# First token block's attention chain in another bank, the filter's mean from one sum, a longer filter, weights loaded a step ahead

## The chip, the core and the metric

One core of a Trainium2 chip runs the kernel. The metric is the device time of one execution in microseconds; the time of a kernel is the median of its runs. TensorE is PE below, VectorE DVE, ScalarE ACT, GpSimd POOL and SyncE SP.

## The reference

One layer over 2048 tokens of 1024 channels, float32. An RMSNorm, one projection to 2816 columns, three mixers side by side, one output projection with the residual, a second RMSNorm, a squared-ReLU MLP with the residual, and a final RMSNorm:

```python
p = h @ w_in                                   # h = rmsnorm(x)
y_a = a_b * _causal_dwconv(a_c * a_h, w_conv_a)         # width 3
g = b_glu[..., :256] * jax.nn.sigmoid(b_glu[..., 256:])
g = _causal_dwconv(g, w_conv_b) + b_conv_b              # width 31
y_b = jax.nn.silu(_layernorm(g, ln_b_g, ln_b_b))        # over 256 channels
# 8 heads of 64, strictly causal, no softmax
z = einsum("bhqd,bhkd->bhqk", qb, kb) * scale
log_beta = log_sigmoid(z); log_1m = where(mask, log_beta - z, 0)
suffix = cumsum(log_1m, axis=3, reverse=True) - log_1m
a = where(mask, exp(log_beta + suffix), 0);  o = a @ vb
x = x + concat([y_a, y_b, y_c]) @ w_out
x = x + square(relu(rmsnorm(x) @ w_ff1)) @ w_ff2;  return rmsnorm(x)
```

## The kernel before, in words

Channels lie on the 128 partitions, tokens along the free axis in four blocks of 512. Each float32 product is made of three matmuls on parts: an operand is split into a rounded part "hi" (ACT copy) and the rest "lo" (a subtraction on DVE or POOL), and `mm3` (lines 99 to 107) adds hi x hi, lo x hi and hi x lo in one bank.

Phase 1 projects. `p_start` makes the first products, then `p_half(0)` treats token blocks 0 and 1 and `p_half(1)` blocks 2 and 3 (numbered by `tb`). Units of 256 columns come in the order G (the width-31 mixer), A (width-3 mixer), K, Q, V. A group of 24 matmuls fills one of three banks "d"; `p_evac` takes it out on DVE (sig, g, ac, u, ya, kq by unit), so the group three later needs the evacuation.

Beside the projections run generators, called sides. `weave` advances each by its share: a tuple says how many units of cost it has, and between which steps of the projections it is spread. A half has some 230 steps.
- `mixer_b`: the width-31 filter, 31 DVE instructions per 128 channels and token block (lines 450 and 452) into the bank "c"; then the LayerNorm: the mean of 256 channels as two matmuls with a constant matrix (line 461), the squares, a column sum (`colsum`), the root on POOL (`rsqrt`, line 118), and its spread back over the partitions by matmuls (`spread`, line 134). A `yield 1.8` separates steps.
- `attention` of token block 0 (i = 0) in half 1. `a_pass1` makes three score tiles z per head (lines 522, 523; ACT's sigmoids at 536 and 537 take them out, POOL masks them) and products R of the complements; `a_cross_a` (lines 610 to 637) turns R over (616), scans it (618), multiplies on (627, 631) and ends with line 635: the transposed products T. `a_pass2` turns T back into the bank "q" (653), multiplies the scores by it (656), splits them and makes eight matmuls "o" with V (701). `attention` runs pass 1 of one head and pass 2 of the one before in turn. Scores and the chain share two banks "z".
- `pre_split` in half 1: 24 pieces of w_out and w1 are loaded raw (five buffers), split into wph and wpl (ACT line 88, POOL line 90; two buffers of wph) and stored for later use.

Phase 2, from some 556 us on, has four blocks of output projection and MLP (`block`), with the attention of token blocks 1 to 3 woven in.

The program's order is not the last word: the framework's scheduler orders the instructions of each engine by its own timing model, and `high_priority` pulls some ahead. Each engine then works in order. DMAs are issued from SP's queue, some from ACT's and POOL's.

Of the kernel before, what the change touches and what calls it, by code (L numbers as in the profile page):

```python
# [7 lines left out]
F32 = mybir.dt.float32  # L8
F32R = mybir.dt.float32r
I32 = mybir.dt.int32  # L10
AF = mybir.ActivationFunctionType
ALU = mybir.AluOpType
# [3 lines left out]
P = 128  # L16
S = 2048
D = 1024
DC = D // P
TB = 512  # L20
H = 8
HD = 64
# [46 lines left out]
class Trunk:  # L69
# [78 lines left out]
    def consts(self, ctx):  # L148
# [6 lines left out]
        nc.scalar.dma_start(t, a["g_attn"].rearrange("(d p) -> p d", p=P))  # L155
# [24 lines left out]
    def vectors(self):  # L180
        nc, tc, a, c = self.nc, self.tc, self.a, self.c
        for name in ("g_ffn", "g_final"):
            t = c.tile([P, DC], F32, name=name)
            self.dma(t, a[name].rearrange("(d p) -> p d", p=P))
            self.gvec[name] = t
        self.wa = c.tile([P, 2, 3], F32, name="wa")
        self.dma(self.wa, a["w_conv_a"].rearrange("(c p) k -> p c k", p=P))
        self.wb = c.tile([P, 2, 31], F32, name="wb")
        self.dma(self.wb, a["w_conv_b"].rearrange("(c p) k -> p c k", p=P))
        self.vb = {}  # L190
        for name in ("b_conv_b", "ln_b_g", "ln_b_b"):
            t = c.tile([P, 2], F32, name=name)
            self.dma(t, a[name].rearrange("(c p) -> p c", p=P))
            self.vb[name] = t
# [246 lines left out]
    def mixer_b(self, hf):  # L441
        nc = self.nc
        for tb in (2 * hf, 2 * hf + 1):
# [13 lines left out]
            for _ in range(3):  # L457
                yield 1.8
            mean = self.psum("ps_mean", "c")
            for c in range(2):  # L460
                nc.tensor.matmul(mean, self.avg, acc[c], start=c == 0, stop=c == 1)
# [11 lines left out]
            for _ in range(4):  # L473
                yield 1.8
# [71 lines left out]
    def a_pass1(self, g):  # L546
# [37 lines left out]
        yield 1  # L584
        tot = self.a_cross_a(g, Rd, None)
# [24 lines left out]
    def a_cross_a(self, g, R, seed):  # L610
# [3 lines left out]
        X = self.ps.tile([P, TB], F32, name="ps_t", tag="z", bufs=self.banks["z"])  # L614
# [24 lines left out]
    def a_pass2(self, g):  # L639
# [39 lines left out]
        tmp = pool.tile([P, TB], F32, name="otmp", tag="om", bufs=ab["om"])[:HD]  # L679
        nc.scalar.activation(tmp, o[HD:P], AF.Copy)  # L680
# [3 lines left out]
        nc.vector.tensor_tensor(self.yc[HD * (h % 2) : HD * (h % 2) + HD], o[0:HD], tmp, op=ALU.add)  # L684
# [27 lines left out]
    def attention(self, groups):  # L712
# [3 lines left out]
        for n in range(len(groups) + 1):  # L716
# [6 lines left out]
            live1, live2 = g is not None, prev is not None  # L723

            lag = 0 if prev and prev["i"] else 2
            while live1 or live2:
                if live2 and (not live1 or (d2 + lag) * max(n1, 1) <= d1 * max(n2, 1)):
                    try:
                        next(p2)
                        d2 += 1  # L730
                        yield 0.5
                    except StopIteration:
                        live2 = False
                elif live1:
                    try:
                        next(p1)
                        d1 += 1
                        yield 0.5
                    except StopIteration:
                        live1 = False  # L740

                if nxt is None and d1 >= 1 and n + 1 < len(groups):
                    nxt = self.a_queries(*groups[n + 1])
                if nxt and "Kd" not in nxt and d1 >= 3:
                    self.a_keys(nxt)
# [19 lines left out]
    def pre_split(self):  # L765

        for name, c, q in self.presplit:
            raw = self.w_raw(self.unit_source(name, c, q))
# [263 lines left out]
    def build(self):  # L1032
        tc = self.tc
        with ExitStack() as ctx:
# [6 lines left out]
            with ExitStack() as c1:  # L1041
# [13 lines left out]
                weave(self.p_half(0), [(Side(self.mixer_b(0)), 115, 20, 225, True), (Side(self.x_norms()), 24, 60, 180, True)])  # L1055
                self.heads = {}
                a0 = Side(self.attention([(h, 0) for h in range(H)]))
                weave(self.p_half(1), [(Side(self.mixer_b(1)), 116, 0, 200, True), (a0, 28, 0, 210, True), (Side(self.pre_split()), len(self.presplit), 0, 200, True)])
# [68 lines left out]
```

## Time and profile before

| what | us |
|---|---|
| median of three runs | 2421.49 (2416.74 to 2425.93) |
| the profiled execution | 2415.74 |
| its span, first to last instruction | 2414.0 |
| PE busy in it | 2379.1 (99%) |
| DVE, ACT, POOL busy | 1534.0, 1043.6, 1128.6 |
| mean granted clock of PE | 0.997 |

Busy time is what the profile records; matmuls overlap, so a busy PE says only that it did not wait. Where an engine waits, the profile names what ended the wait. Times in the timelines count from the span's start.

### The profile page before, as it was taken

What the parts mean: (1) busy time and instruction counts of PE and PEld (TensorE: products, weight loads), DVE (VectorE), ACT (ScalarE), POOL (GpSimd) and SP (SyncE); (2) the same over time, 40 slices, a digit from 0 to 9 for tenths busy, and PEclk for the clock granted to TensorE, in tenths of its full rate; (3) what the DMA queues carried; (4) which work ended last, traced back from release to release, by engine and by line L of the source; (5) the groups of instructions that cost most, each with busy time, mean ns of one, the idle gap of its engine ahead of it and who ended that gap; (6) DMA issues with size and microseconds to landing.
All of it is one profiled execution on the core that took longest, in us unless ns stands there. A gap on an engine that the chain in (4) does not pass through costs nothing.

```text
span 2414.0 us, 32476 instructions
## 1 busy us (share of the span) xinstructions
PE 2379.1 (99%) x11316; PEld 2005.3 (83%) x11316; DVE 1534.0 (64%) x2436; ACT 1043.6 (43%) x1906; POOL 1128.6 (47%) x1133
## 2 busy tenths in 40 slices
PE   8999999999999999999999999999999999999998
PEld 7888877898888888878888888888888888888887
DVE  7966698943898887766676768476667625212114
ACT  5232423342666666544555555355555522121121
POOL 0342477640676666425666665268788720000000
PEclk9999999999999999999999999999999999999999
DMA  7569987789788778687777777866677556655555
GB/s 258 200 234 341 299 269 233 223 265 280 209 225 245 229 206 222 186 300 245 253 234 229 220 242 214 289 200 198 187 202 204 175 183 221 224 187 192 201 183 192
DMA packets 237059, 549.04 MB, mean 227 GB/s; under 512 B 26720, under 2 KB 100448, under 8 KB 218464
## 3 DMA queue, kind: packets, MB, share of 16 engines
q1 hardware_dynamic: 180304, 480.89, 58.9%
q0 software_dynamic: 37504, 56.64, 11.0%
q10 hardware_dynamic: 19088, 9.44, 1.4%
q8 instruction: 89, 1.46, 0.2%
q14 instruction: 74, 0.61, 0.1%
HBM read 390.38 MB, written 148.11 MB: 223 GB/s over the span
## 4 chain that ended last, share of the span: by engine, by line
PE 84%; DMA 6%; DVE 6%; issue 1%; ACT 1%; POOL 1%; SPq 1%; POOLq 0%; DVEq 0%; ACTq 0%
PE ps_y L107 9%; PE ps_y L105 9%; PE ps_y L103 9%; PE ps_u L103 9%; PE ps_u L105 9%; PE ps_u L107 9%; PE ps_p L107 4%; PE ps_p L105 4%; PE ps_p L103 3%; PE ps_z L522 2%; PE ps_z L523 2%; PE ps_x L103 2%; PE ps_x L105 2%; PE ps_x L107 2%; PE ps_o L710 2%; PE ps_o L709 2%
## 5 line engine op out<-in xcount | busy, mean ns | idle before, releaser
L90 POOL TENSOR_TENSOR Alo<-A,Ahi 128x512 fp32r<-128x512 f32 x288 | 385.3, 1347 | 147.0 <-ACT Ahi L88 69.9
L958 DVE TENSOR_TENSOR acc<-acc,ps_y 128x512 f32<-128x512 f32 (+1 forms) x264 | 175.7, 667 | 193.5 <-PE ps_y L107 191.4
L103 PE MATMUL ps_u<-hh,w 128*128 128x512 f32 x1024 | 279.4, 392 | 6.4 <-DMA w<-s_w 6.1
L103 PE MATMUL ps_y<-fh,w 128*128 128x512 f32 (+1 forms) x1056 | 281.2, 384 | 0.0
L105 PE MATMUL ps_y<-fh,w 128*128 128x512 f32 (+1 forms) x1056 | 279.7, 383 | 0.1
L602 POOL TENSOR_TENSOR A<-A,R 128x512 f32<-128x512 f32 x168 | 222.4, 1326 | 121.7 <-ACT A L600 103.3
L107 PE MATMUL ps_y<-fl,w 128*128 128x512 f32 (+1 forms) x1056 | 278.6, 383 | 0.1
L105 PE MATMUL ps_u<-hh,w 128*128 128x512 f32 x1024 | 276.1, 390 | 0.3 <-DVE w L90 0.3
L107 PE MATMUL ps_u<-hl,w 128*128 128x512 f32 x1024 | 275.8, 390 | 0.0
L118 POOL TENSOR_TENSOR rs_y<-rs_v,mhalf 128x4 f32<-128x4 f32 (+1 forms) x13 | 13.2, 1017 | 530.9 <-DVE rs_v L117 486.0
L922 ACT ACTIVATE ps_u<-ps_u 128x512 f32<-128x512 f32 x128 | 74.7, 583 | 399.3 <-PE ps_u L107 399.1
L932 DVE TENSOR_TENSOR fl<-ps_u,fh 128x512 fp32r<-128x512 f32 x128 | 87.7, 685 | 223.3 <-ACT fh L931 222.9
L105 PEld LDWEIGHTS ps_y<-fh,w 128*128 128x128 f32 x1056 | 195.0, 188 | 39.8 <-DMA w<-wraw 0.5
L107 PEld LDWEIGHTS ps_y<-fl,w 128*128 128x128 f32 x1056 | 195.0, 188 | 39.4 <-DVE fl L932 0.6
L88 ACT ACTIVATE Ahi<-A 128x512 fp32r<-128x512 f32 x288 | 176.6, 627 | 117.8 <-PE ps_o L709 51.3
L105 PEld LDWEIGHTS ps_u<-hh,w 128*128 128x128 f32 x1024 | 192.1, 188 | 41.5 <-DVE w L90 0.7
L107 PEld LDWEIGHTS ps_u<-hl,w 128*128 128x128 f32 x1024 | 192.1, 188 | 40.1
L103 PEld LDWEIGHTS ps_y<-fh,w 128*128 128x128 f32 x1056 | 193.6, 188 | 36.8
L103 PEld LDWEIGHTS ps_u<-hh,w 128*128 128x128 f32 x1024 | 186.9, 188 | 42.4 <-DMA w<-s_w 8.1
L604 DVE TENSOR_TENSOR R<-ps_z,R 128x512 f32<-128x512 f32 x168 | 115.7, 689 | 150.6 <-ACT ps_z L601 128.3
L452 DVE SCALAR_TENSOR_TENSOR ps_c<-g,wb,ps_c 128x512 f32<-128x512 f32 x240 | 179.9, 749 | 4.9
L90 DVE TENSOR_TENSOR w<-wraw,w 128x512 fp32r<-128x512 f32 x152 | 150.4, 1008 | 23.7 <-ACT w L88 23.2
(171 smaller groups left out, 4750.7 us busy)
## 6 DMA issues: line engine op xcount, KB each, us to landing
w<-s_w SPq DMA_DIRECT2D x200, 512.0 KB, 3.9
w<-s_w SPq DMA_DIRECT2D x68, 1024.0 KB, 4.8
wraw<-in_w SPq DMA_DIRECT2D x192, 256.0 KB, 5.0
w<-s_w_out SPq DMA_DIRECT2D x64, 512.0 KB, 5.0
s_w<-w SPq DMA_DIRECT2D x32, 1024.0 KB, 5.5
s_w<-w SPq DMA_DIRECT2D x56, 512.0 KB, 4.5
Qd<-KQ SPq DMA_DIRECT2D x64, 256.0 KB, 6.3
xraw<-in_xT SPq DMA_DIRECT2D x48, 256.0 KB, 4.5
```

The lines of the kernel that those rows point to most:

```text
L88: nc.scalar.activation(hi, x, AF.Copy)
L90: e.tensor_tensor(lo, x, f(hi), op=ALU.subtract)
L103: self.nc.tensor.matmul(ps, wh, xh, start=start and k == 0, stop=False)
L105: self.nc.tensor.matmul(ps, wl, xh, start=False, stop=False)
L107: self.nc.tensor.matmul(ps, wh, xl, start=False, stop=stop and k == n - 1)
L452: nc.vector.scalar_tensor_tensor(t, g[:, k : k + TB], self.wb[:, c, k : k + 1], t, op0=ALU.mult, op1=ALU.add)
L522: nc.tensor.matmul(z[:, oc], keys, g["qh"][:, qc], start=k == 0, stop=False)
L602: nc.gpsimd.tensor_tensor(t, t, R, op=ALU.mult)
L604: nc.vector.tensor_tensor(Rn, z, R, op=ALU.mult)
L922: nc.scalar.activation(ps, ps, AF.Relu)
L932: nc.vector.tensor_tensor(lo, ps, f(hi), op=ALU.subtract)
L958: nc.vector.tensor_tensor(acc[d][:, cols], acc[d][:, cols], ps, op=ALU.add)
```

## The change

Five edits in phase 1, and one in pass 2 of every head.
1. The vectors are laid out by row on the host, so that each partition's values lie together in memory.
2. The mean of the width-31 mixer: POOL adds the two tiles of 128 channels, and one matmul takes the sum. One more step ahead of the mean, two more ahead of the spread; the side's units and spans in `weave` grow with it.
3. For i = 0 the chain's tile ps_t lies in the bank "q" in place of "z", and `a_cross_a` of a head is put behind the end of the previous head's pass 2.
4. Pass 2 copies the upper half of o straight into yc and adds the lower half there; the tile otmp goes.
5. `pre_split` asks for the raw weights of the next piece before it splits this one.

```diff
@@ vectors (consts, vectors; on the host)
-        nc.scalar.dma_start(t, a["g_attn"].rearrange("(d p) -> p d", p=P))
+        nc.scalar.dma_start(t, a["g_attn"])
-            self.dma(t, a[name].rearrange("(d p) -> p d", p=P))
+            self.dma(t, a[name])
...
-        "g_attn": lay(np.asarray(inputs["g_attn"])[0]),
+        "g_attn": lay(np.asarray(inputs["g_attn"])[0].reshape(DC, P).T),
...
@@ mixer_b
-            for _ in range(3):
+            both = self.mx.tile([P, TB], F32, name="sum", tag="sq", bufs=2)
+            nc.gpsimd.tensor_tensor(both, acc[0], acc[1], op=ALU.add)
+            for _ in range(4):
                 yield 1.8
             mean = self.psum("ps_mean", "c")
-            for c in range(2):
-                nc.tensor.matmul(mean, self.avg, acc[c], start=c == 0, stop=c == 1)
+            nc.tensor.matmul(mean, self.avg, both, start=True, stop=True)
...
-            for _ in range(4):
+            for _ in range(6):
                 yield 1.8
             R = self.spread(yv, "c")
@@ a_pass1
+        if not i:
+
+            while not g["free"]():
+                yield None
         tot = self.a_cross_a(g, Rd, None)
@@ a_cross_a
-        X = self.ps.tile([P, TB], F32, name="ps_t", tag="z", bufs=self.banks["z"])
+        X = self.psum("ps_t", "z" if g["i"] else "q")
@@ a_pass2
-        tmp = pool.tile([P, TB], F32, name="otmp", tag="om", bufs=ab["om"])[:HD]
-        nc.scalar.activation(tmp, o[HD:P], AF.Copy)
...
-        nc.vector.tensor_tensor(self.yc[HD * (h % 2) : HD * (h % 2) + HD], o[0:HD], tmp, op=ALU.add)
+        y = self.yc[HD * (h % 2) : HD * (h % 2) + HD]
+        nc.scalar.activation(y, o[HD:P], AF.Copy)
+        nc.vector.tensor_tensor(y, y, o[0:HD], op=ALU.add)
@@ attention
+            if g:
+                g["free"] = lambda: not live2
...
-                if live2 and (not live1 or (d2 + lag) * max(n1, 1) <= d1 * max(n2, 1)):
+                if live2 and (not live1 or d1 > n1 or (d2 + lag) * max(n1, 1) <= d1 * max(n2, 1)):
...
-                        next(p1)
+                        if next(p1) is None:
+
+                            d1 = n1 + 1e-3
+                            continue
@@ pre_split
-        for name, c, q in self.presplit:
-            raw = self.w_raw(self.unit_source(name, c, q))
+        nxt = self.w_raw(self.unit_source(*self.presplit[0]))
+        yield 1
+        for n, (name, c, q) in enumerate(self.presplit):
+            raw = nxt
+            if n + 1 < len(self.presplit):
+                nxt = self.w_raw(self.unit_source(*self.presplit[n + 1]))
@@ build
-                weave(self.p_half(0), [(Side(self.mixer_b(0)), 115, 20, 225, True), (Side(self.x_norms()), 24, 60, 180, True)])
+                weave(self.p_half(0), [(Side(self.mixer_b(0)), 130, 20, 225, True), (Side(self.x_norms()), 24, 60, 180, True)])
-                weave(self.p_half(1), [(Side(self.mixer_b(1)), 116, 0, 200, True), (a0, 28, 0, 210, True), (Side(self.pre_split()), len(self.presplit), 0, 200, True)])
+                weave(self.p_half(1), [(Side(self.mixer_b(1)), 130, 0, 224, True), (a0, 28, 0, 212, True), (Side(self.pre_split()), len(self.presplit) + 1, 0, 205, True)])
```

How the change moves instructions is told by the engines' orders. First DVE in half 1, at the second evacuation "u" (ps_p to u, line 355), before; ps_c is the filter's sum, R a product of the head in work, ac and ca belong to the width-3 mixer:

```order
L575 TENSOR_TENSOR R<-om 128x256
L452 SCALAR_TENSOR_TENSOR ps_c<-g_2_2890,wb,ps_c 128x512
L349 TENSOR_TENSOR ac<-ps_p,R 128x512
L452 SCALAR_TENSOR_TENSOR ps_c<-g_2_2890,wb,ps_c 128x512 x11
L355 TENSOR_TENSOR u_3_3266<-ps_p,ac 128x512
L452 SCALAR_TENSOR_TENSOR ps_c<-g_2_2890,wb,ps_c 128x512
L580 TENSOR_TENSOR R<-om,R 128x256
```

The same place on DVE in the changed kernel, the last twelve rows up to "u"; ahead of them stand ac, the two products R (581, 583), the transposition of R into ps_t (621) and four filter steps between them:

```order
L623 SCALAR_TENSOR_TENSOR T<-d_90,ps_t 128x512
L452 SCALAR_TENSOR_TENSOR ps_c<-g_2_2886,wb,ps_c 128x512
L626 MEMSET ps_t 32x16
L452 SCALAR_TENSOR_TENSOR ps_c<-g_2_2886,wb,ps_c 128x512
L632 TENSOR_TENSOR ps_t<-ps_t,T 32x16
L452 SCALAR_TENSOR_TENSOR ps_c<-g_2_2886,wb,ps_c 128x512
L632 TENSOR_TENSOR ps_t<-ps_t,T 32x16
L452 SCALAR_TENSOR_TENSOR ps_c<-g_2_2886,wb,ps_c 128x512
L632 TENSOR_TENSOR ps_t<-ps_t,T 32x16
L452 SCALAR_TENSOR_TENSOR ps_c<-g_2_2886,wb,ps_c 128x512
L636 TENSOR_TENSOR tot<-ps_t,T 32x16
L355 TENSOR_TENSOR u_3_3249<-ps_p,ac 128x512
```

The chain of a head that stood behind this "u" now stands ahead of it, and between ac and "u" there are nine filter steps in place of eleven.

Then ACT behind the same "u", before; ut keeps the last two columns of u, wph is the rounded part of weights split ahead, om and A are the sigmoids that take a score tile out of its bank:

```order
L356 ACTIVATE ut<-u_3_3266 128x2
L88 ACTIVATE wph<-wraw 128x512
L680 ACTIVATE otmp<-ps_o 64x512
L88 ACTIVATE wph<-wraw 128x512 x3
L536 ACTIVATE om<-ps_z 128x512
L537 ACTIVATE A_3333<-ps_z 128x512
```

The same place on ACT in the changed kernel:

```order
L356 ACTIVATE ut<-u_3_3249 128x2
L88 ACTIVATE wph<-wraw 128x512
L688 ACTIVATE yc<-ps_o 64x512
L537 ACTIVATE om<-ps_z 128x512
L538 ACTIVATE A_3329<-ps_z 128x512
L88 ACTIVATE wph<-wraw 128x512 x2
```

The sigmoids of the score tile now stand behind one split, no longer behind four.

Last SP's queue at the first pieces of `pre_split`, before; wraw are raw loads, s_w_out the stores of the split pieces, Qd a load of queries:

```order
L79 DMA wraw<-in_w_out 128x512 x5
L79 DMA s_w_out<-wph 128x512 x2
L79 DMA Qd<-KQ 64x4x256
L79 DMA s_w_out<-wpl 128x512
L79 DMA Qd<-KQ 64x4x256
L79 DMA wraw<-in_w_out 128x512
```

and in the changed kernel:

```order
L79 DMA wraw<-in_w_out 128x512 x5
L79 DMA s_w_out<-wph 128x512 x2
L79 DMA Qd<-KQ 64x4x256 x2
L79 DMA s_w_out<-wpl 128x512
L79 DMA wraw<-in_w_out 128x512
```

Five raw loads stand ahead of the first store in both.

## Rows read from the trace of the kernel before

**Rows 1.** The page: busy us, share of the span, instructions.

```profile
PE 2379.1 (99%) x11316; PEld 2005.3 (83%) x11316; DVE 1534.0 (64%) x2436; ACT 1043.6 (43%) x1906; POOL 1128.6 (47%) x1133
```

**Rows 2.** Windows: us, busy us of each engine, granted clock, DMA share, GB/s.

```profile
287.14:355.57 68.43, 63.97 (x292) 52.29 (x291) 67.30 (x95) 21.63 (x43) 50.08 (x51) 0.98 0.88 295
355.57:416.06 60.49, 54.96 (x255) 44.44 (x256) 53.46 (x81) 20.06 (x38) 48.07 (x51) 0.97 0.75 239
...
275.00:400.00 125.00, 115.00 (x527) 93.36 (x526) 116.07 (x164) 42.84 (x87) 94.98 (x97) 0.97 0.82 270
400.00:475.00 75.00, 75.00 (x357) 62.91 (x356) 72.36 (x115) 22.51 (x38) 52.34 (x60) 1.00 0.71 222
```

**Rows 3.** Waits of PE, 275 to 400 us: us in total, times, longest.

```profile
PE ps_z L522 <- DVE T L635: 3.4, 1, 3.4
PE ps_z L522 <- ACT A L537: 2.7, 1, 2.7
PE ps_R L134 <- POOL rs_y L118: 1.7, 1, 1.7
PE ps_p L103 <- DVE u L355: 1.0, 1, 1.0
...
PE ps_mean L461 <- ACT cb L456: 0.4, 1, 0.4
```

**Rows 4.** Timeline of PE: start, us, what [idle before, releaser].

```profile
325.42 0.39 PE L522 MATMUL ps_z<-Qd,Kd 128*128 128x256 f32 x1 [3.35 <-DVE T L635]
...
326.75 3.52 PE L107 MATMUL ps_p<-xl,wh 128*128 128x512 f32 x8
...
361.70 1.98 PE L103 MATMUL ps_p<-xh,wh 128*128 128x512 f32 x8
366.36 0.39 PE L522 MATMUL ps_z<-Qd,Kd 128*128 128x256 f32 x1 [2.68 <-ACT A L537]
...
366.95 3.06 PE L105 MATMUL ps_p<-xh,wl 128*128 128x512 f32 x8
```

**Rows 5.** Timeline of ACT around 364 us.

```profile
364.05 1.15 ACT L88 ACTIVATE wph<-wraw 128x512 fp32r<-128x512 f32 x2 [6.52 <-issue]
```

**Rows 6.** Timeline of SP's queue around 358 us, and the DMA issues.

```profile
357.58 0.32 SPq L79 DMA_DIRECT2D Y<-ya  x1
...
358.47 0.90 SPq L79 DMA_DIRECT2D s_w<-wph  x2
...
s_w<-wph SPq DMA_DIRECT2D x8, 256.0 KB, 5.5
```

**Rows 7.** The chain (start, us, what) at the mean; line 469 on POOL.

```profile
121.54 1.82 PE ps_mean L461 x4
...
L469 POOL TENSOR_TENSOR sq<-sq x4: 1288/1292/1300, 128.0 to 490.4; 128x512 f32<-128x512 f32 x4
```

**Rows 8.** DVE: line 580 (min/median/max ns), chain's timeline, groups to 560 us (busy, ns).

```profile
L580 DVE TENSOR_TENSOR R<-om,R x32: 406/620/4208, 284.8 to 1876.9; 128x256 f32<-128x256 f32 x32
...
317.79 0.72 DVE L616 STREAM_TRANSPOSE ps_t<-R 128x512 f32<-128x512 f32 x1
319.04 1.20 DVE L618 TENSOR_TENSOR_SCAN T<-d,ps_t 128x512 f32<-128x512 f32 x1
324.69 0.68 DVE L635 TENSOR_TENSOR T<-T,ps_t 128x512 f32<-128x512 f32 x1
...
L452 DVE SCALAR_TENSOR_TENSOR ps_c<-g,wb,ps_c 128x512 f32<-128x512 f32 x120 | 89.7, 747 | 2.1
...
L627 DVE TENSOR_TENSOR ps_t<-ps_t,T 32x16 f32<-32x16 f32 x24 | 4.4, 183 | 0.8
```

**Rows 9.** The start: timeline of ACT, and DMA issues (KB, us to landing).

```profile
4.92 0.72 ACT L223 ACTIVATE xh<-xraw,g_attn 128x512 fp32r<-128x512 f32 x1 [0.43 <-DMA g_attn<-in_g_attn]
...
g_attn<-in_g_attn ACTq DMA_DIRECT2D x1, 4.0 KB, 4.1
b_conv_b<-in_b_conv_b SPq DMA_DIRECT2D x1, 1.0 KB, 2.1
```

More of the change, by code (lines that the diff above doesn't have):

```diff
@@ L183, in vectors @@
             t = c.tile([P, DC], F32, name=name)
-            self.dma(t, a[name].rearrange("(d p) -> p d", p=P))
+            self.dma(t, a[name])
             self.gvec[name] = t
         self.wa = c.tile([P, 2, 3], F32, name="wa")
-        self.dma(self.wa, a["w_conv_a"].rearrange("(c p) k -> p c k", p=P))
+        self.dma(self.wa, a["w_conv_a"])
         self.wb = c.tile([P, 2, 31], F32, name="wb")
-        self.dma(self.wb, a["w_conv_b"].rearrange("(c p) k -> p c k", p=P))
+        self.dma(self.wb, a["w_conv_b"])
         self.vb = {}
@@ L192, in vectors @@
             t = c.tile([P, 2], F32, name=name)
-            self.dma(t, a[name].rearrange("(c p) -> p c", p=P))
+            self.dma(t, a[name])
             self.vb[name] = t
@@ L1108 @@
         ),
-        "g_attn": lay(np.asarray(inputs["g_attn"])[0]),
-        "w_conv_a": lay(np.asarray(inputs["w_conv_a"])[0].T),
-        "w_conv_b": lay(np.asarray(inputs["w_conv_b"])[0].T),
-        "b_conv_b": lay(np.asarray(inputs["b_conv_b"])[0]),
-        "ln_b_g": lay(np.asarray(inputs["ln_b_g"])[0]),
-        "ln_b_b": lay(np.asarray(inputs["ln_b_b"])[0]),
-        "g_ffn": lay(np.asarray(inputs["g_ffn"])[0]),
-        "g_final": lay(np.asarray(inputs["g_final"])),
+        "g_attn": lay(np.asarray(inputs["g_attn"])[0].reshape(DC, P).T),
+        "w_conv_a": lay(np.asarray(inputs["w_conv_a"])[0].reshape(3, 2, P).transpose(2, 1, 0)),
+        "w_conv_b": lay(np.asarray(inputs["w_conv_b"])[0].reshape(31, 2, P).transpose(2, 1, 0)),
+        "b_conv_b": lay(np.asarray(inputs["b_conv_b"])[0].reshape(2, P).T),
+        "ln_b_g": lay(np.asarray(inputs["ln_b_g"])[0].reshape(2, P).T),
+        "ln_b_b": lay(np.asarray(inputs["ln_b_b"])[0].reshape(2, P).T),
+        "g_ffn": lay(np.asarray(inputs["g_ffn"])[0].reshape(DC, P).T),
+        "g_final": lay(np.asarray(inputs["g_final"]).reshape(DC, P).T),
     }
```

## The prediction

> **What bounds the kernel now.** I read the page first: TensorE (PE) is busy for 99% of the span, and no other engine comes near it [rows 1]. So only two things can change the time: matmuls that are added or removed, and the few microseconds in which PE waits or runs at the lower clock. The windows by stage show where those are [rows 2]. The order of instructions changes up to the first third of block 0 and is the old one behind it, so I count nothing there. From 400 to 475 us PE does not wait at all. In the 125 us from 275 to 400, the first half of the projections of tokens 1024 to 2047, where the attention of the first token block is woven in, PE is busy for 115.0: 10.0 us of waiting. The reader should also see VectorE (DVE) in this stretch: busy for 116.1 of 125 us, and for 72.4 of 75 in the next.
>
> The waits view names the causes [rows 3], the timelines show their places. The score matmul at 325.4 waits 3.35 us for line 635, the last step of the chain on the transposed products, which holds one of the two banks "z"; the eight projection matmuls behind it take 3.52 us, where eight take 1.98 us elsewhere [rows 4], because the granted clock falls after a long wait (its mean in the two halves of the stretch is 0.98 and 0.97 [rows 2]; full speed is 2.4 GHz, the lower level 1.2): 1.54 us more. The score matmul at 366.4 waits 2.68 us, and the matmuls behind it take 3.06 instead of 1.98: 1.08 more. So the stretch loses 10.0 + 2.6 = 12.6 us, some 0.5% of the kernel.
>
> Why is the second one late? It waits for a sigmoid on ScalarE (ACT) that frees its bank. ACT stood still for 6.52 us ahead of two splits "wph" [rows 5], and the sigmoids stood behind them. The trace gives no releaser ("issue"). A split needs its raw weights and a free "wph" (two buffers, freed when the store of the piece two earlier lands). The stores "s_w<-wph" left SyncE (SP) only at 358.47, behind the store of "ya" at 357.58 [rows 6], and such a store takes a median of 5.5 us: 364.0, which is when ACT went on. So it was the store, not the load. And with one bank held by the chain, the score matmul had nowhere else to go.
>
> **The change part by part.**
>
> The mean. Line 461 issues two full-precision matmuls per token block, four records of PE; such a group takes 1.82 us of PE in the chain [rows 7]. One matmul of the sum makes it 0.91. Four blocks: 4 x 0.91 = **3.6 us less on PE**, at every place without slack. In exchange GpSimd (POOL) gets four adds of 128x512; its nearest row is line 469, 1.29 us [rows 7]. POOL is busy 47% [rows 1]; the add has the step of 1.8 that was added for it, so on PE's path I count 0. If that cover fails, PE waits at the mean for one add, 1.3 us at most per block, two of them in the dense stretch: 0 to 2.6 us.
> The row that gives me pause is line 580 on DVE: a product of two SBUF tiles of 256 columns takes 0.41 us at least and 4.21 us at most [rows 8], and the longest one stands just ahead of the 3.35 us wait. No row says which engine held it. The Trainium skill (SBUF — State Buffer, "Who interferes with whom") says that a DVE instruction with two SBUF inputs and a GpSimd instruction that reads SBUF block each other for the whole instruction, whichever comes second; by that rule each of the four new adds can hold DVE up for its 1.29 us, and the sum would be up to 2.6 us longer in the dense half. By the rows alone a slow product costs DVE, and PE only where DVE is the bound: I count 0 here, and the 2.6 us of a late add stay as the upper end.
>
> The chain's bank. For the first token block the transposed products move from "z" (two banks) to "q" (one). The chain then no longer takes a bank from the scores: the waits of 3.35 and 2.68 us lose their cause. In "q" it alternates with ps_q, which DVE alone writes and reads, so in-order DVE adds no wait there; the new wait for the end of pass 2 only changes the program's order. But I do not count the 3.35 + 1.54 us as won. From 287.1 to 355.6 us DVE is busy for 67.3 of 68.4 us [rows 2]: it is the bound of these nine projection groups, and at the end of it PE already waits 1.0 us for DVE's evacuation "u" of the group three before [rows 3]. If PE comes 4.9 us earlier it waits there 4.9 us longer. Worse, the change puts the chain ahead of this very "u" (order of DVE above): two filter steps fewer, 2 x 0.75, but two products (0.41 each at best), transposition 0.72, scan 1.20, three small products 0.18 each, two still smaller ones 0.2 [rows 8]: 3.5 - 1.5 = 2.0 us more DVE work before it. So this first part costs between 0 (some of DVE's stretched products get shorter) and +2.0 us; I take **+1.0**.
> Behind 356 us it is otherwise: DVE has gaps (53.5 busy of 60.5 us [rows 2]), and up to the first "kq" evacuation the change's order has five filter steps fewer (3.8 us) and one transposition more (0.7): 3 us less work. Here the waits fall away: 2.68 + 1.08 us at 366 (ACT's order above: one split instead of four between the evacuation's copy and the sigmoid), 0.4 at the mean (its filter is one step older) and 1.7 at line 134, where PE waits for POOL's rs_y [rows 3] and the change gives two steps more. These four are 5.8 us; the clock of 0.97 over 60 us [rows 2] is worth 1.8 us, of which the 1.08 are a part, so I take **6.5 us less**. The other waits of the stretch, some 0.9 us, stay.
>
> Weights a step ahead. In SP's order five raw loads stand ahead of the first store before and after the change: the five buffers already allowed it, the scheduler already did it. The wait of 6.5 us on ACT was for a store. **0.**
>
> The longer filter. Half 0: 115 units over 205 steps become 130; half 1: 116 over 200 become 130 over 224, the same pace 0.58. Half 0 is denser, but in DVE's order the work ahead of each evacuation of that half changes by under 2 us, and no wait of PE there is among the causes above. 0. In half 1 the second block's filter ends some 20 us later, beside the projection V behind 475 us, which DVE has little to do for. 0.
>
> yc without the extra tile: one ACT copy and one DVE add as before, 0. The vectors laid out by row: xh waited 0.43 us for g_attn [rows 9], whose load took 4.1 us; loads of a fourth of its elements land in 2.1. PE's first matmul comes **0.4 us earlier**; the others hide behind matmuls (0).
>
> Sum: -3.6 + 1.0 - 6.5 - 0.4 = **-9.5 us**, 2406.2 against the profiled execution's 2415.74 (span 2414.0 and 1.7 around it). That execution is 5.75 us below the median of the three runs, 2421.49; so I predict 2421.49 - 9.5 = **2412.0 us**, 0.39% less.
>
> **The rivals.**
> *All waits of the stretch go*, because the chain in "q" lets PE run ahead and DVE's stretched products shrink with POOL's new order: 3.6 + 12.6 + 0.4 = 16.6 us, 2404.9. For it: line 580 has a record of 4.21 us where 0.41 is possible [rows 8]. Against: DVE's 67.3 of 68.4 us.
> *Only the matmuls go.* Each wait comes back as one for an evacuation, or the spread of line 134 waits longer, since its sums and it now stand only 24 projection matmuls apart (three rows of 1.98 us [rows 4], 5.9 us): -3.6 - 0.4 and nothing else, 2417.5. For it: DVE's 97% up to 475 us.
> *Slower.* "q" has one bank, and the chain starts only behind the previous head's last product. If DVE runs late, pass 2 of the head has no ps_q, its eight "o" matmuls stand at the head of PE's queue, and PE waits as it did at 325 us: 3.35 + 1.54 = 4.9 us for each of the seven heads behind the first, 34 us, against 16.6 won: +17.7, 2439. It decides from the point where the chain's time in the bank (7.6 us from line 616 at 317.8 to the end of line 635 at 325.4, filter steps between [rows 8]) and the pass 2 behind it take more than the distance of two score groups in the change's order, 48 projection matmuls, at 1.98 us for eight [rows 4] 11.9 us.
> *The bank does nothing*, since DVE is the bound throughout: that is the second rival.
>
> **How the numbers follow.** Forecast (6 to 12 us less) 0.42, all waits 0.27, only the matmuls 0.24, slower 0.07. A measurement tells about 0.5% here, 12.1 us. "All waits" lies beyond it, and the forecast's edge: faster 0.29. The slower rival lies beyond it on the other side almost wholly: 0.06. Same: 0.65. The range takes in all waits gone (2404.9), the spread of the runs (4.7 us below their median) and a little more, 2399, and at the other end only the matmuls (2417.5) with 2.6 us for the adds and the spread above (4.4): 2424.
>
> **What would show it.** In the changed profile: eight PE records of the mean instead of sixteen; no score matmul waiting for the chain in the first token block; PE's waits between 275 and 400 us down from 10.0 to 4 to 8 us, most of them now ps_p for an evacuation on DVE; no score matmul waiting for a sigmoid. The first matmul near 5.8 us. I am wrong if "o" matmuls wait for the products, if the spread of line 134 waits over 3 us, or if these waits vanish altogether.

## The result, and the profile after

The changed kernel is slower: 2429.03 us (15 runs, 2423.7 to 2435.55) against 2421.49 (15 runs), a ratio of 1.0034 (interval 1.0022 to 1.0045). I had predicted 2412.0 with a range up to 2424. The profiled execution has a span of 2424.6 us, 10.6 more than that of before. Among the executions of e1, e5 and e11 below, three at a granted clock of 0.65 and one of 5244 us are left out of the ratios, not of the medians.

The first line of the page of the changed kernel shows that PE has no less to do:

```profile
PE 2379.4 (98%) x11308; PEld 2009.6 (83%) x11308; DVE 1549.1 (64%) x2436; ACT 1044.8 (43%) x1906; POOL 1133.8 (47%) x1137
```

Eight matmuls fewer than in [rows 1], as meant, and still the same busy time: PE's records got slower somewhere, and 10.3 us were added in which it does nothing. The windows of the changed kernel (us, busy us of PE, its weight loads, DVE, ACT, POOL; granted clock, DMA share, GB/s) say where:

```profile
300.00:325.00 25.00, 21.97 (x106) 18.16 (x105) 24.47 (x34) 7.75 (x16) 20.13 (x21) 1.00 0.88 288
325.00:350.00 25.00, 20.98 (x86) 17.18 (x85) 24.93 (x26) 7.66 (x16) 18.37 (x20) 0.86 0.72 216
...
375.00:400.00 25.00, 17.11 (x80) 13.64 (x78) 22.90 (x26) 7.40 (x14) 18.06 (x17) 0.96 0.74 241
400.00:425.00 25.00, 24.68 (x114) 21.01 (x115) 19.99 (x34) 6.34 (x11) 20.78 (x24) 0.90 0.69 219
...
556.00:620.00 64.00, 60.06 (x277) 50.64 (x278) 34.60 (x52) 25.24 (x46) 20.41 (x25) 0.97 0.95 282
```

From 275 to 400 us PE is idle for 16.1 us where it was for 10.0 [rows 2], DVE is fuller than before (119.6 us of 125 against 116.1), and the granted clock falls in three windows, in or behind those in which PE waits. And 556 to 620 us, which had no idle time before, has 3.9 us. The bill: 3.5 us less for the mean (line 462 takes 4.2 us, line 461 took 7.7). Idle time: 6.4 us more between 275 and 475 us, 4.5 more between 500 and 620, 2.0 less behind that, and 1.6 more behind 720 us; 10.5 in all. Slower records: PE's busy time is 0.3 us above that of before with 3.5 us of work less, so 3.8 us; by the windows, what is missing to a clock of 1.00 is 8.9 us against 3.5, 5.4 more. With the 3.8 the bill is +10.8, against 10.6 measured.

The waits of PE in the changed kernel, 275 to 425 us, and then 500 to 720 us (total us, times, longest):

```profile
PE ps_ss L127 <- POOL sq L470: 6.8, 1, 6.8
PE ps_o L706 <- DVE yc L689: 4.0, 1, 4.0
PE ps_o L706 <- ACT Ahi L88: 3.0, 1, 3.0
PE ps_mean L462 <- POOL sum L458: 1.5, 1, 1.5
PE ps_o L706 <- POOL Alo L90: 0.6, 1, 0.6
PE ps_p L103 <- DVE u L355: 0.5, 1, 0.5
```

```profile
PE ps_x L103 <- DMA w<-s_w_out: 2.4, 1, 2.4
PE ps_v L397 <- DVE vt L405: 2.1, 1, 2.1
```

Not one wait of [rows 3] for the chain or for a sigmoid is left: these went as forecast. New ones stand in their place, larger, and the two in the second fence are where I had counted nothing. The places below show how they come about.

**The wait of 4.0 us.** The timeline of DVE ahead of it, then POOL's at the same time:

```profile
329.91 6.22 DVE L576 TENSOR_TENSOR R<-om 128x256 f32<-128x256 f32 x1
336.05 0.74 DVE L452 SCALAR_TENSOR_TENSOR ps_c<-g,wb,ps_c 128x512 f32<-128x512 f32 x1
336.71 0.67 DVE L689 TENSOR_TENSOR yc<-yc,ps_o 64x512 f32<-64x512 f32 x1
```

```profile
329.71 1.30 POOL L350 TENSOR_TENSOR ac<-ac,R 128x512 f32<-128x512 f32 x1
330.97 1.29 POOL L90 TENSOR_TENSOR Alo<-A,Ahi 128x512 fp32r<-128x512 f32 x1
332.22 1.28 POOL L90 TENSOR_TENSOR wpl<-wraw,wph 128x512 fp32r<-128x512 f32 x1
333.47 0.71 POOL L574 TENSOR_TENSOR A<-A,om 128x256 f32<-128x256 f32 x1
334.15 1.25 POOL L90 TENSOR_TENSOR wpl<-wraw,wph 128x512 fp32r<-128x512 f32 x1
335.36 1.23 POOL L83 DMA_DIRECT2D Kd<-KQ  x2
```

A DVE product that takes 0.41 us where nothing is in its way [rows 8] takes 6.22, as long as POOL goes from one instruction on SBUF straight to the next: here five of them, up to the DMA issue at 335.36. Behind it stands the addition yc, which frees the one bank "o", and in PE's order the eight matmuls "o" of the next head stand ahead of the projection:

```profile
337.43 0.58 PE L706 MATMUL ps_o<-Ahi,Vd 128*128 128x256 f32 x1 [4.02 <-DVE yc L689]
...
339.31 3.61 PE L103 MATMUL ps_p<-xh,wh 128*128 128x512 f32 x8
```

Eight matmuls then take 3.61 us in place of 1.98. The whole group of these products, lines 567 to 583, 275 to 475 us (busy us, mean ns | idle before):

```profile
L581 DVE TENSOR_TENSOR R<-om,R 128x256 f32<-128x256 f32 x6 | 16.3, 2716 | 1.3 <-POOL om L542 1.3
L576 DVE TENSOR_TENSOR R<-om 128x256 f32<-128x256 f32 x7 | 12.2, 1749 | 1.3 <-POOL om L542 1.3
L583 DVE TENSOR_TENSOR R<-om,R 128x256 f32<-128x256 f32 x6 | 7.6, 1273 | 0.0
L567 DVE TENSOR_TENSOR R<-om 128x256 f32<-128x256 f32 x7 | 5.6, 795 | 1.7 <-POOL om L542 1.7
```

41.7 us for 26 products; before it was 33.1 for 28. At 0.41 us each it would be 11.

The two other long waits lead back to such products too. DVE ahead of the wait of 6.8 us, which ends at 400.32, and POOL's squares; then DVE and ACT ahead of the 3.0 us, which end at 317.54:

```profile
378.65 6.40 DVE L581 TENSOR_TENSOR R<-om,R 128x256 f32<-128x256 f32 x1 [1.33 <-POOL om L542]
385.08 2.66 DVE L583 TENSOR_TENSOR R<-om,R 128x256 f32<-128x256 f32 x1
...
396.16 0.68 DVE L465 TENSOR_TENSOR cb<-cb,ps_mean 128x512 f32<-128x512 f32 x1
...
398.55 1.71 POOL L470 TENSOR_TENSOR sq<-sq 128x512 f32<-128x512 f32 x1
```

```profile
306.43 5.24 DVE L581 TENSOR_TENSOR R<-om,R 128x256 f32<-128x256 f32 x1
...
316.87 0.61 ACT L88 ACTIVATE Ahi<-A 128x512 fp32r<-128x512 f32 x1
```

From the first product to the subtraction of the mean DVE has hardly a gap, so its two products bring the squares 8.2 us later than two of 0.41 us would; POOL's own order adds some 1.0 us, since ACT had the second tile ready at 397.55 and two splits "wpl" stood ahead of the squares. In the other place DVE goes without a gap from the product to the evacuation "sig" at 314.60, which ACT waited 9.38 us for, with the split "Ahi" behind it. So 13.8 of the 16.4 us of waits stand behind products of 5 to 6 us.

**The waits at 557 and 577 us.** The last store of the mixer leaves POOL at 543.73 us, before it was 517.43. It is read back for block 0, and ACT's splits "y" of that block stand ahead of the evacuations vt in ACT's order. POOL's row, then ACT's:

```profile
543.73 1.13 POOL L485 DMA_DIRECT2D Y<-sq  x2
```

```profile
553.37 2.71 ACT L88 ACTIVATE y<-yraw 128x512 fp32r<-128x512 f32 x5 [6.06 <-DMA Y<-sq]
555.99 0.81 ACT L404 ACTIVATE vt<-ps_v,rs_y 128x256 fp32r<-128x256 f32 x2
```

ACT stands for 6.06 us with the evacuations behind it, and PE waits 2.1 us for one. SP's queue, too, stands from 543.8 until 554.75 for these splits to free a raw buffer, with loads for block 0 behind it.

### The profile page after: what moved, and what is told of

Same layout as the page of the kernel before. It is cut to its first block, busy times and chain, and to the rows that moved or that the text cites. A ratio compares the mean times of both kernels' runs of the same rounds, so it can differ in the third digit from the quotient of the medians.

```text
span 2424.6 us, 32448 instructions
## 1 busy us (share of the span) xinstructions
PE 2379.4 (98%) x11308; PEld 2009.6 (83%) x11308; DVE 1549.1 (64%) x2436; ACT 1044.8 (43%) x1906; POOL 1133.8 (47%) x1137
## 3 DMA queue, kind: packets, MB, share of 16 engines
q0 software_dynamic: 37504, 56.64, 10.9%
## 4 chain that ended last, share of the span: by engine, by line
PE 86%; DMA 6%; DVE 4%; issue 2%; POOL 2%; ACT 0%; SPq 0%; POOLq 0%; DVEq 0%; ACTq 0%
PE ps_y L103 10%; PE ps_y L107 9%; PE ps_y L105 9%; PE ps_u L103 9%; PE ps_u L105 9%; PE ps_u L107 9%; PE ps_p L103 4%; PE ps_p L107 4%; PE ps_p L105 4%; PE ps_z L523 2%; PE ps_z L524 2%; PE ps_o L715 2%; PE ps_o L714 2%; PE ps_x L103 2%; PE ps_x L105 2%
```

## The experiments

Theory A: the products of DVE stand behind runs of POOL instructions, whatever waits for DVE next pays, and the change only moved that. Its rivals: B, the single bank; C, the sum for the mean; D, the later end of the filter. Each run stands beside runs of the kernel before on the same chip. A difference of two runs that did not run beside each other is marked (apart); such a difference of medians can move by 1 to 2 us when it is taken from the ratios instead. The waits are those of PE from 275 to 475 us, the products are the sum of the four lines there, both of the profiled execution (before: 10.0 and 33.1; changed: 16.4 and 41.7).

| run | us | ratio to before (interval) | waits | products (count) |
|---|---|---|---|---|
| e1_z_bank, e15 | 2424.7 | 1.0009 (1.0000 to 1.0018) | 11.8 | 38.0 (28) |
| e2_two_means | 2428.1 | 1.0022 (1.0011 to 1.0033) | 12.2 | 40.7 (25) |
| e3_act_copy | 2409.0 | 0.9945 (0.9933 to 0.9958) | 1.5 | 20.5 (27) |
| e4_mean_alone | 2427.0 | 1.0021 (1.0013 to 1.0030) | 10.9 | 31.3 (28) |
| e5_old_filter | 2420.7 | 0.9991 (0.9981 to 1.0001) | 14.7 | 38.4 (26) |
| e6_q_alone | 2418.0 | 0.9983 (0.9974 to 0.9992) | 6.7 | 27.4 (28) |
| e7_split_dma | 2435.5 | 1.0053 (1.0033 to 1.0072) | 16.8 | 25.0 (26) |
| e8_old_filter_dma | 2431.1 | 1.0034 (1.0022 to 1.0047) | 17.0 | 23.9 (25) |
| e9_before_act_copy | 2409.0 | 0.9955 (0.9940 to 0.9969) | 4.5 | 28.2 (28) |
| e10_sum_alone | 2424.1 | 1.0014 (1.0004 to 1.0024) | 16.6 | 34.4 (26) |
| e11_pool_copy, e16 | 2423.9 | 1.0011 (1.0000 to 1.0023) | 6.5 | 38.8 (28) |
| e12_no_mixer | 2420.6 | 0.9996 (0.9987 to 1.0006) | 9.8 | 33.8 (28) |
| e13_early_split | 2410.7 | 0.9949 (0.9929 to 0.9968) | 2.5 | 16.6 (23) |
| e14_fewer_split | 2415.0 | 0.9967 (0.9954 to 0.9980) | 7.1 | 27.5 (28) |
| e17_sum_early_split | 2413.0 | 0.9963 (0.9950 to 0.9977) | 1.0 | 16.5 (20) |
| e18_early_twelve | 2420.5 | 0.9999 (0.9988 to 1.0010) | 1.3 | 17.1 (24) |

The waits and products of e1 and e11 come from e15 and e16, profiles of the same kernels. e3, e9, e11 and e16 leave out the low part of the weights split ahead, so they are prices and not versions to use.

**GpSimd's subtractions: e3 and e9.**

```diff
 pre_split
-            self.split(hi, lo, raw, "pool")
+            self.nc.scalar.activation(hi, raw, AF.Copy)
+            self.nc.scalar.activation(lo, raw, AF.Copy)
```

> The changed kernel with the 24 subtractions wpl of the weights split ahead left out of GpSimd: ScalarE writes a copy there instead, so the low part of these weights is not computed. 24 instructions of 1.3 us leave GpSimd, 24 of 0.6 us come to ScalarE. Theory A: no product of lines 567 to 583 over 2.5 us between 275 and 475 us, their sum under 25 us, PE's waits from 275 to 425 us under 5 us, 2409 to 2417 us. Theory B: the 'o' matmuls still wait for VectorE's order, 5 us and more, 2423 to 2428 us. Theory C: the mean and the squares still wait, 2423 to 2429 us.

> The kernel before with the 24 subtractions wpl left out of GpSimd (ScalarE writes a copy, so the low part of these weights is not computed), as in the run that did this to the changed kernel and took 20 us off it. With it the change can be priced with and without GpSimd's runs. Theory A (the loss is the products that stand behind GpSimd): this gains less than 20, about the 12.6 us of waits and slow clock in the stretch, 2409 to 2412 us, and the change is worth nothing to 3 us less there. If the change costs the same with and without these subtractions: 2401 to 2403 us, 20 us under before as well.

With the subtractions gone both kernels take 2409.0 us. The costliest of the four groups of products in the changed kernel was line 581; in e3 it is

```profile
L581 DVE TENSOR_TENSOR R<-om,R 128x256 f32<-128x256 f32 x7 | 3.2, 454 | 0.0
```

Its mean falls from 2716 ns to 454, the longest product of the stretch from 6.40 us to 1.45, and 16.4 us of waits become 1.5. So 20 us of the changed kernel, 12 of the one before, hang on 24 POOL instructions that PE never waits for by name. For the changed kernel this is theory A, with the three waits above. For the kernel before it is shown less well: in e9 the products only fall from 33.1 to 28.2 us, two of 4.63 and 3.75 us remain, and still 5.5 us of waits and 11.8 us of time go. A rival is left there that no run separates: without the subtraction POOL is free earlier, and the split pieces are stored and their buffers free earlier, on which, by my reading, the wait of 2.68 us before the change hung. Without these subtractions the change as a whole is worth nothing that can be told (apart); e3 still has theory D's waits, 5.8 us between 500 and 620 us.

**The bank: e6, and e1 with e15.**

```diff
 e1: the changed kernel, a_pass1 without the wait for g["free"], and in a_cross_a
-        X = self.psum("ps_t", "z" if g["i"] else "q")
+        X = self.psum("ps_t", "z")
 e6: the kernel before, with the change's edits to a_pass1, a_cross_a and attention alone
```

> The kernel before with only the chain's bank changed: the transposed products of the first token block in q, behind the end of pass 2. My sum for this part: +1.0 and -6.1 us or so, 2416 us. Theory A: VectorE stays the bound, the waits for z become waits of the 'o' matmuls, 2419 to 2425 us. Theory B (the bank itself costs the 4.4 us by which the first run was under the changed kernel): 2425 to 2428 us. The waits at 557 and 577 us should not be there.

> The changed kernel with the chain of the first token block back in the bank z and without the wait for the end of pass 2; the rest of the change stays. Theory A (VectorE products of two SBUF tiles, lines 567 to 583, stand behind runs of GpSimd instructions, 41.7 us for 26 of them between 275 and 475 us against 33.1 for 28 before, and whoever waits for VectorE next pays): the waits only change their name, from 'o' for line 689 or a split to 'z' for the chain, 2423 to 2430 us. Theory B (the single bank and the later chain let the 'o' matmuls wait, 7.6 us and the lower clock behind them): those go, 2417 to 2420 us. Theory C (the mean from a sum costs it: 1.5 us for the add, 6.8 for the squares): nothing changes, 2427 to 2431 us.

> A second look at the changed kernel with the chain back in z (2424.7 us in the timed runs), for its profile. Theory A: waits of 10 us and more between 275 and 475 us, now of score matmuls for line 640 or for a sigmoid, and products of more than 30 us in sum; theory D: the waits at 557 and 577 us are there as in the changed kernel. 2421 to 2430 us.

Alone the bank is a gain of 4.3 us, near the 5.5 of my sum; PE's waits in the dense half of e6 are

```profile
PE ps_mean L461 <- ACT cb L456: 3.7, 1, 3.7
PE ps_o L705 <- DMA wraw<-in_w: 2.6, 1, 2.6
PE ps_o L705 <- ACT Ahi L88: 0.4, 1, 0.4
```

In the changed kernel the same edit is a loss: undone, it gives 4.4 us back (2429.0 to 2424.7, apart). There the waits of the "o" matmuls become 6.8 us of score matmuls for a sigmoid, and the sum of waits falls from 16.4 to 11.8. An edit that is worth -4.3 us in one company and +4.4 in another has no price of its own: theories A and B both named part of it, and neither bound holds by itself.

**The sum: e10, e2 and e4.** e10 is the kernel before with the add and one matmul, and nothing else; e4 has the new steps and spans as well; e2 is the changed kernel with two matmuls and no add.

```diff
 e2, mixer_b
-            both = self.mx.tile([P, TB], F32, name="sum", tag="sq", bufs=2)
-            nc.gpsimd.tensor_tensor(both, acc[0], acc[1], op=ALU.add)
...
-            nc.tensor.matmul(mean, self.avg, both, start=True, stop=True)
+            for c in range(2):
+                nc.tensor.matmul(mean, self.avg, acc[c], start=c == 0, stop=c == 1)
```

> The kernel before with the mean as one matmul of a sum made on GpSimd, all steps and spans of the filter as before. My sum: 3.6 us less and a wait of 0 to 2.6 us, 2418 to 2420 us. Theory D (the later end of the filter made the run with steps and spans 5.1 us slower than before): no wait at 557 and 577 us, 2418 to 2421 us. Theory C (the sum is what costs in the dense half): waits for the sum and the squares of 5 us and more, 2423 to 2427 us.

> The changed kernel with the mean as two matmuls again and no add on GpSimd; the added steps and the longer filter stay. PE gets 3.6 us more of matmuls. Theory A: two adds of 1.3 us fewer on GpSimd in the dense half, so little of the products' 41.7 us goes: 2428 to 2433 us. Theory B: 3.6 us more than the changed kernel, 2432 to 2433 us. Theory C: the waits of 1.5 and 6.8 us go, 2422 to 2426 us.

> The kernel before with the mean from one sum, its three added steps and the longer filter alone. My sum counted 3.6 us less of matmuls and no wait: 2417 to 2418 us. Theory A: two adds more among GpSimd's runs; the products grow by 0 to 4 us, 2417 to 2422 us. Theory B: the mean is not the cause, 2417 to 2419 us. Theory C: the mean and the squares wait as in the changed kernel, 8 us less the 3.6, 2425 to 2428 us.

The sum saves 3.5 us of matmuls and never shows them: alone it costs 3.3 us, and in the changed kernel its undoing makes no difference that can be told (0.9 us less, apart). PE's waits in e10:

```profile
PE ps_z L523 <- ACT A L538: 6.1, 1, 6.1
PE ps_z L523 <- DVE T L636: 4.4, 1, 4.4
PE ps_ss L127 <- POOL sq L470: 3.2, 1, 3.2
PE ps_o L702 <- ACT Ahi L88: 2.5, 1, 2.5
```

Theory C's wait for the squares is there with 3.2 us (6.8 in the changed kernel, 6.4 in e5, 2.0 in e4; e2, e6 and e12, without the sum, have none, but e14, without it too, has 1.6). More of the waits in e10 are the old score waits, grown, and its two longest products are 7.03 and 6.59 us, where the longest before was 4.21. e4 took the time that theory C foresaw, but 2.0 us of its 10.9 are for the squares. So that the sum alone costs 3.3 us is shown; that its waits are C's is not, since the 6.8 us of the changed kernel lead back to held products. Whether the add itself or the order that the scheduler makes of it lengthens them stays open.

**The filter's end: e5.**

```diff
 mixer_b: 3 steps ahead of the mean, 4 ahead of the spread, as before
-weave(self.p_half(0), [(Side(self.mixer_b(0)), 130, 20, 225, True), ...
+weave(self.p_half(0), [(Side(self.mixer_b(0)), 115, 20, 225, True), ...
-weave(self.p_half(1), [(Side(self.mixer_b(1)), 130, 0, 224, True), ...
+weave(self.p_half(1), [(Side(self.mixer_b(1)), 116, 0, 200, True), ...
```

> The changed kernel with the mixer's steps (3 ahead of the mean, 4 ahead of the spread) and the filter's units and spans of before; the mean is still one matmul of a sum. Theory D (the filter ends 24 steps later, its last store leaves at 543.7 instead of 517.4 us, SyncE's queue stands behind the load that reads it back until 554.8, and TensorE waits 2.1 us for vt and 2.4 us for w, with the lower clock behind them): no wait between 500 and 620 us, 4.5 + 1.9 us less than the changed kernel, 2422 to 2424 us. Theory A alone (only VectorE's products behind GpSimd in the dense half cost it): the same number of GpSimd instructions there, 2427 to 2431 us. If the add gets too few steps, TensorE waits up to 1.3 us more at each of two means: 2425 to 2427 us.

8.3 us less (apart), more than the 6.4 of theory D, and no idle time of PE between 500 and 620 us; e4 and e2, which keep the spans, still have 5.2 and 5.4 us of it. In the dense half 14.7 us of waits stay. D is shown as a part of its own beside A, though e5 takes the added steps back together with the spans. Its size is less sure: e8 against e7, which differ by the same edits and ran beside each other, gives 4.4 us, and e4 against e10 2.9 (apart). So some 3 to 8 us by the medians.

**What is left: e12.** The changed kernel with e2's and e5's edits together, so bank, vectors, yc and loads.

> The changed kernel without everything that concerns the mixer: two matmuls for the mean, its steps, units and spans as before. What is left is the bank q, the vectors by row, the copy straight into yc and the loads a step ahead. With the bank alone the kernel took 2418.0 us. By my sum the other three are worth 0.4 us: 2417 to 2419 us. If the loads a step ahead or yc cost something among the changed kernel's waits: 2421 us and more. If the sum is what costs 2.7 us in the run with the old filter: 2416 to 2419 us.

2.6 us above e6 (apart), where I had 0.4 below. The two intervals overlap, and the products sum to 33.8 against 27.4: the three small edits gave nothing that can be told, and whether they cost something is not settled. The wait for yc is here too, 3.8 us behind a product of 6.22 us, though this kernel has neither the sum nor the longer filter; e6 has it not. The start did move: in the changed kernel's profile xh waits for its data and the first matmul comes at 6.33 us (before: 6.21), but here it comes at 5.82, and in eight of the ten profiles used here with the vectors by row at 5.4 to 5.8, where it is 6.1 to 6.5 without. g_attn landed in 2.9 to 3.9 us there, not in 2.1.

**Another engine for the subtraction: e7, e8, e11 and e16.** e7 is the changed kernel with an accumulating DMA in place of the subtraction (ACT writes the negated part first), e8 the same in e5; e11 and e16 let POOL copy one tile.

```diff
 e7, e8
-            self.split(hi, lo, raw, "pool")
+            self.split_dma(hi, lo, raw)
 e11, e16
+            self.nc.scalar.activation(hi, raw, AF.Copy)
+            self.nc.gpsimd.tensor_copy(lo, raw)
```

> The changed kernel with the low parts of the weights split ahead made by an accumulating DMA instead of a subtraction on GpSimd (ScalarE writes the negated rounded part first): the same weights, 24 instructions of 1.3 us on GpSimd become 24 DMA issues. Theory A: as in the run with the copy on ScalarE, products under 2.5 us, 2409 to 2415 us. If a GpSimd DMA issue holds VectorE as a subtraction does, 24 x 0.6 us in place of 24 x 1.3: half of the 20 us, 2417 to 2421 us. If the DMA rings of this stretch (0.72 to 0.98 busy) cannot take 12 MB more, stores and loads come late: 2425 us and more.

> The two edits of the other runs together: the old steps and spans of the filter, and the weights split ahead by an accumulating DMA. Theories A and D both: 2429 less 15 to 20 and less 5 to 6, 2403 to 2409 us, faster than the kernel before by over 0.5%. Theory A without D: 2409 to 2414 us. Theory D without A: 2422 to 2424 us.

> The changed kernel in which GpSimd makes wpl by a copy of one tile instead of a subtraction of two (the low part of these weights is then not the difference). It asks whether it is the number and length of GpSimd's instructions that holds VectorE or their second operand. If any GpSimd instruction on SBUF holds a VectorE product and the copy is as long as the subtraction (1.3 us): products as in the changed kernel, 40 us for 26, 2425 to 2432 us. If the copy is shorter or holds nothing: products under 2.5 us and 2409 to 2416 us.

> A second look at the changed kernel in which GpSimd copies one tile in place of the subtraction of two (2423.9 us in the timed runs), for its profile. If one SBUF tile read is enough to hold VectorE: the copies stand in rows with long products, 35 to 42 us in sum. If not: products as short as without GpSimd's subtractions, some 20 us, and the 5 us gained come from there. 2419 to 2430 us.

e7 missed theory A's range by 20 us and e8 that of both theories by 22: the products are short (25.0 and 23.9 us), but ACT's timeline in e7, in order, now stands for stores with sigmoids and splits behind it,

```profile
331.51 0.63 ACT L95 ACTIVATE wpl<-wraw 128x512 fp32r<-128x512 f32 x1 [5.57 <-DMA s_w_out<-wpl]
...
342.60 0.63 ACT L95 ACTIVATE wpl<-wraw 128x512 fp32r<-128x512 f32 x1 [6.95 <-DMA s_w_out<-wpl]
343.17 0.63 ACT L97 ACTIVATE wph<-wraw 128x512 fp32r<-128x512 f32 x1
343.71 0.61 ACT L88 ACTIVATE Ahi<-A 128x512 fp32r<-128x512 f32 x1
```

so that "o" matmuls wait 13.6 us for splits. e16 says what holds a product: POOL's copies read one tile and are half as long,

```profile
L786 POOL CAST wpl<-wraw 128x512 fp32r<-128x512 f32 x24 | 15.0, 629 | 35.4 <-DMA s_w_out<-wpl 14.7 <-issue 13.1 <-DMA s_w<-wpl 7.0
```

and the products still sum to 38.8 us for 28. One of them, on DVE, and the middle four of POOL's six rows meanwhile:

```profile
396.70 5.33 DVE L567 TENSOR_TENSOR R<-om 128x256 f32<-128x256 f32 x1
```

```profile
398.05 0.63 POOL L542 TENSOR_SCALAR_AFFINE_SELECT om<-om 128x512 f32<-128x512 f32 x1
398.62 0.62 POOL L542 TENSOR_SCALAR_AFFINE_SELECT A<-A 128x512 f32<-128x512 f32 x1
399.19 0.60 POOL L786 CAST wpl<-wraw 128x512 fp32r<-128x512 f32 x1
399.76 0.73 POOL L565 TENSOR_TENSOR A<-A,om 128x256 f32<-128x256 f32 x1
```

Three of these read one tile only, and the product did not get in between. PE's waits there fall to 6.5 us, though, and 5.5 us of waiting for the sum come behind 475 us: the time gained (5.1 us, apart) does not come from shorter products. So the sum of the products alone does not order the runs; what stands behind a long one must count too, which no run measures on its own.

**Fewer subtractions in the dense half: e13, e14, e17, e18.** All four compute the low parts of these weights. e13 is e6 with 8 of the 24 pieces in the first half:

```diff
+                ps = Side(self.pre_split())
-                weave(self.p_half(0), [(Side(self.mixer_b(0)), ...
+                weave(self.p_half(0), [(ps, 8, 90, 190, False), (Side(self.mixer_b(0)), ...
-..., (Side(self.pre_split()), len(self.presplit), 0, 200, True)])
+..., (ps, len(self.presplit) - 8, 0, 200, True)])
```

e18 moves 12 over the steps 90 to 220; e14 is e6 with PRE = 0, so that 8 pieces are split in block 0; e17 is e5 with 8 moved.

> The kernel before with the chain in q alone (2418.0 us), and 8 of the 24 pieces of weights split ahead moved from the dense half into the first half, where GpSimd is busy for 21 of 50 us at 100 to 150 us. Theory A: a third of GpSimd's subtractions leave the dense half; without all of them it was worth 11 to 20 us, so a third 4 to 6 us of the 7 that wait there: 2411 to 2415 us. If their loads, stores and buffers (shared with the loads of x) make the first half wait: 2418 to 2425 us.

> The kernel before with the chain in q alone (2418.0 us), and only 16 of the 24 pieces split ahead: the 8 pieces of w1 are split in block 0 like the rest of w1. Theory A: a third of the subtractions leave the dense half, 4 to 6 us less, 2412 to 2414 us, if block 0 hides 8 splits more on VectorE, which is busy for 84.5 of 100 us there. If block 0 does not hide them: 8 x 1.0 us or less come back, 2418 to 2422 us.

> The changed kernel with the old steps and spans of the filter (2420.7 us) and 8 of the 24 pieces of weights split ahead moved into the first half. The same without the mean from a sum, the loads a step ahead, yc and the vectors took 2410.7 us. Theory A: with room on GpSimd and VectorE the sum keeps its 3.6 us, 2406 to 2409 us. If the add on GpSimd costs its matmuls again wherever the mean stands in the dense half: 2410 to 2415 us.

> The kernel before with the chain in q, and 12 in place of 8 pieces moved into the first half (8 gave 2410.7 us, with 2.5 us of waits left between 275 and 475 us and 3.3 us of new ones before 275). Theory A: up to 2 us less in the dense half; the first half's new waits grow by half, 1.6 us: 2409 to 2413 us. If the first half's buffers are full: over 2414 us.

e13 is the fastest version that computes all weights, 0.51% under the kernel before (0.32% to 0.71%). Its stretch of 275 to 400 us:

```profile
275.00:400.00 125.00, 122.51 (x580) 101.63 (x579) 107.19 (x168) 39.96 (x79) 84.70 (x88) 1.00 0.74 250
```

Against [rows 2] PE has 7.5 us more of work in it and the clock does not fall. The longest product in it is 1.15 us. e14, whose 8 pieces go to block 0, gains 3.0 us over e6 (apart), less than the 4 to 6 expected. e18 shows the other end, 2420.5 us, the case that I had named for full buffers: the dense half is as good, but the first half's waits grow, 5.7 us of them one wait for POOL's squares. e17 keeps the sum, and with it the loads, yc and the vectors: 2413.0 us against 2410.7 in e13 (apart), so even with room in the dense half the 3.6 us of the sum do not show; 3.1 us of its waits are one for the squares in the first half.

## Why the prediction was wrong, point by point

- *The mean, 3.6 us less on PE*: the matmuls measured 3.5 less. The other half of the step, "on PE's path I count 0" for the add, failed: 1.5 us at one mean in the changed kernel, and +3.3 us in all where the sum stood alone (e10). My upper end, 2.6 us, was too small. I took POOL at its 47% of the whole span, where [rows 2] had it busy for 95.0 of the 125 us that the add had to fit into.
- *The row that gives me pause*: the rule was right and my weighing was not. I wrote that "by the rows alone a slow product costs DVE, and PE only where DVE is the bound: I count 0 here", and in the next paragraph DVE is busy for 67.3 of 68.4 us. And I priced by the rule one POOL instruction of 1.29 us per product. The rule of the Trainium skill (SBUF — State Buffer, "Who interferes with whom") agrees with the trace on who is held, but the trace goes further: the product stood for a run of five, 6.22 us. This is the step that failed first: held products, put at 0, stand ahead of 13.8 us of waits, and with 24 of the POOL instructions gone 20 us went (e3).
- *The chain's bank, +1.0 and -6.5*: alone it measured -4.3 (e6), so the mechanism was right and the sum nearly. The waits for the chain and for a sigmoid went as forecast. In the changed kernel the "o" matmuls took the place of the score matmuls, the sign of being wrong that I had named: 7.6 us of waits, and only 0.5 for an evacuation, where I had expected most. Why the same edit is a loss there is not shown. The sum and the later filter alone do not make it so: the "o" matmuls wait 7.0 us without the sum (e2), 6.2 without the later filter (e5) and 5.0 without either (e12).
- *The longer filter, 0*: this is the second step that failed. I saw the end move by some 20 us (measured 26) and asked only whether DVE had room there. What stood behind it was a store, its reading back, and ACT's splits in order ahead of the evacuations: 4.5 us of waits and the clock behind them, 3 to 8 us when undone (e5, e8, e4).
- *Weights a step ahead, yc, the vectors, -0.4*: the 0.4 at the start was right by the first matmul of most profiles, though not in the changed kernel's own. In the time it is not seen; against e6, e12 leaves the three together at 2.6 us more, where the intervals overlap.
- *The rivals*: the slower rival had the right engine and place, "o" matmuls waiting behind a late DVE, and the wrong extent: two waits of 3.0 and 4.0 us, not seven of 4.9. Its chance of 0.07 came of pricing it only as all or nothing.
- The sum as a whole treated each wait as a price tag on one edit. In the dense half DVE is full and its held products move with the order of POOL, so the variants put the loss on different waits: 7 to 17 us with all 24 subtractions on POOL in that half, 1 to 7 with fewer or none. e7 and e8 are another matter: no subtraction, and 17 us of waits, mostly for ACT's splits and what hangs on them. That all of it is one budget of DVE is my reading; e16, with long products and 6.5 us of waits, does not fit it.

## What to carry to other kernels

Where one engine is at 97% in a stretch, look for its instructions whose longest record is ten times the shortest, and find what ran on the other engine during them, before pricing any wait by name: taking 24 POOL instructions out of the stretch was worth 12 and 20 us here, more than any other edit. When a side stream is stretched so that it ends later, follow its last store to the load that reads it back, and see what stands behind that load's user in order.

## What the runs showed of the hardware

A DVE product of two SBUF tiles can stand for a whole run of POOL instructions, not for the one that it met: 6.22 us beside five of them, 6.40 us in another place, there across a DMA issue of POOL at 382.83, and 7.03 us in e10; 0.41 us is the least. POOL instructions that read a single tile, selects and copies, do not let it in between either (5.33 us in e16).
